# A two-layer encoder's Fourier layer: the place of gate products, norms, spectrum splits and spectrum loads in the queues

## The chip, the core and the metric

One core of a Trainium2 chip runs the whole kernel. The metric is the time of one execution in microseconds on the device, as the median of several runs. The engines are named as in the profile: PE (TensorE, matmuls; PEld is its weight load), DVE (VectorE), ACT (ScalarE), POOL (GpSimd) and SP (SyncE, which here only issues DMAs).

## The reference

Two sequences, x_prompt (2048 x 1024) and x_sample (512 x 1024), go through the same two layers and a final RMSNorm.

```python
def attention_layer(x, ...):                    # layer 0: windowed attention, gated, projected
    h = rmsnorm(x, g)
    z = h @ w_in                                # q, k, v, gate
    o = banded_gqa_with_sink(q, k, v, rel_bias, sink)
    return x + (o * silu(gate)) @ w_out

def fourier_layer(x, g, w_gate, w_out):         # layer 1: the change lies here
    h = rmsnorm(x, g)
    hg = h.reshape(b, s, 4, 256)                # four channel groups
    f = fftn(hg, axes=(1, 3), norm="ortho").real
    gate = h @ w_gate
    return x + (f.reshape(b, s, d) * silu(gate)) @ w_out

# and at the end
return rmsnorm(x, final_norm)
```

All is float32. Matmuls are made of three products of split operands (`matmul3`, L92): high by high, high by low, low by high, where a "split" is a high part copied by ACT and a low part that DVE subtracts.

## The kernel before

The attention layer runs first, up to about 1060 us of the profile, and leaves its result x1 in HBM. The change does not touch it. The Fourier layer, whose first channel DFT starts at 1064.2 us, then runs in these steps.

**Gates.** The 20 tiles of 128 rows are taken in ten pairs (`pairs`). For each pair `gates` (L1104) makes the gate projection of both tiles with seven block products instead of eight, in three PSUM accumulators W, Z and X, and sums them in the SBUF tile c: c11, c12 and c22. Between the products it calls hooks, which do the next pair's transposes, its channel DFT (`z`) and, for the last pair, the first steps of what follows. `silu` (L1115) turns a sum into a gate and POOL stores it to HBM (s2d). At the end of each group of four tiles `combine` runs a radix-4 step over the tiles (L1183) on DVE; the results are the spectra of the positions' first stage, kept in HBM (gsd, evd, odd).

**Positions.** `position` (L1325) is the second DFT stage for one output residue k1. It splits the spectrum (`halves_of`, L1313: two halves of 512 columns, and a real and a sine part for all but k1 = 0 and 8), multiplies it with a table into a cosine sum A and a sine sum B for each half hf, and puts them together on DVE: L1353 to L1356 add and subtract the sine sum. L1356 is the last reader of the sine sum of its half. B has one PSUM bank for both halves, so B's matmuls of the second half wait for L1356 of the first. At the end L1358 multiplies with the gate, 1024 columns at a time, for one or two output tiles (k1 and its mirror).

**Outputs.** `finish` (L1376) transposes the product, projects it with 48 matmuls to two PSUM accumulators (fo), adds them to x1 (L1384) and calls `normed` (L1365): a sum of squares on ACT (L979), a power on POOL (L89), a product of 1024 columns on DVE (L1368), a store on SP. For the last five residues `Outs` (L1389) does the projection with seven products for two tiles, as the gates do: Wo, Zo and Xo, with sums L1449, between which hooks run the next residue's position.

**Order of the work.** The sample (512 rows) comes first: s1 inside the last pair's gates (tiles us, As, Bs), then s0 and s2; then the prompt's residues p0 and p8, p4, p2, p6, p1, p7, p3 and p5. Between them DVE builds the spectra by radix steps (L1181, L1630, L1632): the even ones before p2, the odd ones (g1 to g7) while p2 and p6 run. The spectra of p7, p3 and p5 are stored by ACT (god) and read back by `reads` (L1656) into the tiles go, one residue ahead. A scheduler orders each engine's queue by its own estimate of times and by the dependencies; `after` (L135) gives it a dependency without a semaphore, so that one instruction is placed behind another. So a small edit can move instructions that the diff doesn't name.

The lines and names of the prediction: W, Z, X (gate accumulators), c22 (L1152), us and up (position results of the sample and the prompt), gs and gp (their split spectra), As and Ap, Bs and Bp (cosine and sine sums), tru and tr (transposes), w32f (the output weights as loaded), wo (their split).

Of the kernel before, what the change touches and what calls it, by code (L numbers as in the profile page):

```python
# [42 lines left out]
def encoder(  # L43
# [886 lines left out]
    def fourier_phase(tail):  # L930
        with ExitStack() as es:
# [15 lines left out]
            def zt(name):  # L947
                return right([P, D], F32, name)
# [134 lines left out]
                        ACT.activation(out, v[:, 1], AF.Copy, scale=scale)  # L1083
                        last_z[0] = DVE.scalar_tensor_tensor(out, v[:, 0], scale, out, ALU.mult, ALU.add)

            last_z = [None]

            def prod(out, a, b, ks, first):

# [14 lines left out]
            def gates(pr, hooks):  # L1104
# [44 lines left out]
                hook(3)  # L1149
                x_step(2)  # L1150
                prod(W, S[3], wg["T3"], four, False)
                DVE.tensor_tensor(c22, c22, W, ALU.add)  # L1152
                silu(c22, 1, 1)
                hook(4)
                x_step(3)
# [166 lines left out]
                        out.append(t)  # L1322
                return out

            def position(name, tab, gr, gs, tiles, loads=None, parts=None, between=None):  # L1325

                s2s, tb = loads or position_loads(name, tab, tiles)
                cs, sn, ns = [(tb[:, 2 * i], tb[:, 2 * i + 1]) for i in range(3)]
                bp = bank(f"B{name}")
                us = [zt(f"u{name}_{i}") for i in range(len(tiles))]  # L1330
                for hf in range(2):
                    ts = parts[hf] if parts else halves_of(name, gr, gs, hf)
                    if hf and between:
                        between()

                    def acc(out, tabs, c0, n):
                        for i, (w, t) in enumerate(zip(tabs, ts)):
                            v = [
                                t[:, part].rearrange("p (g c) -> p g c", g=2)[:, :, c0 : c0 + n]
                                for part in range(2)  # L1340
                            ]
                            matmul3(out, w, v, i == 0, i == len(ts) - 1)

                    a = bank(f"A{name}_{hf}")[:, :260].rearrange("p (g c) -> p g c", g=2)
                    acc(a, (cs, ns), 0, 130)
                    b = bp[:, hf * 256 : hf * 256 + 256].rearrange("p (g c) -> p g c", g=2)
                    acc(b, (sn, cs), P, P)
                    uv = [u.rearrange("p (g c) -> p g c", g=4)[:, 2 * hf : 2 * hf + 2] for u in us]
                    ACT.copy(uv[0][:, :, 0 : P + 1], a[:, :, 0 : P + 1])
                    re, im = uv[0][:, :, 1:P], b[:, :, 1:P]  # L1350
                    for v in uv[1:]:
                        ACT.copy(v[:, :, 0 : P + 1 : P], a[:, :, 0 : P + 1 : P])
                        DVE.tensor_tensor(v[:, :, 1:P], re, im, ALU.add)  # L1353
                        DVE.tensor_tensor(v[:, :, P + 1 : 256], re, im, ALU.subtract)
                    DVE.tensor_tensor(uv[0][:, :, P + 1 : 256], re, im, ALU.add)
                    DVE.tensor_tensor(re, re, im, ALU.subtract)  # L1356
                for u, s2 in zip(us, s2s):
                    DVE.tensor_tensor(u, u, s2, ALU.mult)  # L1358
                return list(zip(us, tiles))

            def out_rows(r):
# [3 lines left out]
            def normed(x2, r):  # L1365

                inv = sumsq(x2, f"f{r[0]}")
                DVE.scalar_tensor_tensor(x2, x2, inv[:, 0:1], gfb, ALU.mult, ALU.mult)  # L1368
                SP.dma_start(out_rows(r), x2)

            def residual(r):
# [155 lines left out]
                return name, 4 * k1, gl[0], gl[1] if len(gl) > 1 else None, tiles, (s2s, tb)  # L1527

            POOL.dma_start(mir, mirror)
            first, early, wo, w32f = [], [], [], []  # L1530

            def f_load(k):
                if k < 4:
# [18 lines left out]
            def turn_first(i):  # L1552
# [5 lines left out]
                0: [lambda: f_load(0)],  # L1558
                1: [lambda: f_load(1), lambda: early.append(sample(0, (0,), (left,), (xtile,), left))],
                2: [lambda: f_load(2), lambda: early.append(sample(2, (1,), (left,), (xtile,), left))],  # L1560
                3: [lambda: first.extend(position(*one)), lambda: f_load(3)],
                4: [lambda: f_load(4)],
                5: [lambda: turn_first(0), lambda: f_load(5)],
                6: [lambda: turn_first(1)],
            })
# [14 lines left out]
            G = {}  # L1580
# [59 lines left out]
            g1r, g7r = pm(e0c, o0c, "g1r")  # L1640
            g1s, g7s = pm(o0s, e0s, "g1s")
            g3r, g5r = pm(e1c, o1s, "g3r")
            g5s, g3s = pm(o1c, e1s, "g5s")
            G[1], G[7], G[3], G[5] = (g1r, g1s), (g7r, g7s), (g3r, g3s), (g5r, g5s)
            for k1 in (7, 3, 5):
                for t, g in zip(god[k1], G[k1]):
                    ACT.dma_start(t, g)
            o = Outs(6, position("p6", 6, *G[6], pair(6, 16, 0)))
            f_sums("T1", right)
            f_sums("T2", right)  # L1650
            finish(*pend.pop(0))
# [3 lines left out]

            def reads(k1):  # L1656

                gl = []
                for i, src in enumerate(god[k1]):
                    g = zt(f"go{k1}_{i}")  # L1660
                    SP.dma_start(g, src)
                    gl.append(g)
                return gl, table(f"p{k1}", k1, left)

            nxt = {"r": (G[1], table("p1", 1, left))}
            for k1, k2 in ((1, 7), (7, 3), (3, 5), (5, None)):
# [3 lines left out]
                def split_g():  # L1670

                    nxt["s"] = [gated(name, r, place) for r, place in zip(tiles, (xtile, left))]
                    nxt["p"] = [halves_of(name, *gl, hf) for hf in range(2)]
                    if not ft["T3"]:
                        f_sums("T3", right)

                def transform(third):
                    if not ft["N4"]:
                        f_sums("N4", left)
                    nxt["o"] = Outs(k1, position(name, k1, None, None, tiles, (nxt["s"], tb), nxt["p"], third))  # L1680

                def turns():
                    nxt["o"].operands()
# [108 lines left out]
```

## Time and profile before

| | |
|---|---|
| timed runs | 1588.07, 1588.2, 1588.9 us; median 1588.2 |
| profiled execution | 1587.64 us, its span 1585.9 us |
| granted TensorE clock | 0.999 |
| PE busy | 1572.4 us, 99% of the span |
| DVE, ACT, POOL busy | 1151.0 (73%), 876.4 (55%), 446.5 us (28%) |
| moved by DMA | 373.88 MB, 236 GB/s on average |

The span is the time from the first to the last instruction of the profiled execution; the time of the same execution is a little longer. PE's row says that it has an instruction in work for nearly the whole span. The waits of an engine, listed by who ended them, tell where its remaining idle time comes from, and the timeline gives the start and the duration of each group of instructions, with the idle time before it and what ended it in brackets.

### The profile page before, as it was taken

How to read it: one execution, taken by the hardware profiler on the slowest of the kernel's cores; microseconds unless marked ns; L12 is line 12 of the kernel's file. 1: busy time of each engine (PE TensorE's matmuls, PEld its weight loads, DVE VectorE, ACT ScalarE, POOL GpSimd, SP SyncE). 2: the span in 40 equal slices, each digit the busy share in tenths (PEclk: the TensorE clock that was granted, in tenths of full speed). 3: DMA queues.
4: the chain of work that ended last, by engine and by line, in shares of the span. 5: the costliest groups of instructions: out<-in, count | busy, mean ns of one | idle time of the engine just before them, and what ended most of it. 6: DMA issues, size and time to landing. Idle time of an engine off the chain costs nothing. (4 is left out here: it accounts for less than half of the span.)

```text
span 1585.9 us, 27430 instructions
## 1 busy us (share of the span) xinstructions
PE 1572.4 (99%) x9743; PEld 1320.2 (83%) x9743; DVE 1151.0 (73%) x2785; ACT 876.4 (55%) x2089; POOL 446.5 (28%) x613
## 2 busy tenths in 40 slices
PE   9999999999999999999999999999999999999998
PEld 7778888888898888988888888888888888888886
DVE  5788665887548786378764577669878878889796
ACT  6688634677237684257852476646655554343342
POOL 2566651421403414024222242223112111111110
PEclk9999999999999999999999999999999999999999
DMA  7587696665865567656649656675557469548752
GB/s 288 205 311 282 237 350 211 228 237 199 294 224 205 208 249 257 238 196 229 242 168 334 217 209 225 247 252 199 207 200 262 176 224 406 180 173 313 265 205 80
DMA packets 100579, 373.88 MB, mean 236 GB/s; under 512 B 12139, under 2 KB 22379, under 8 KB 83036
## 3 DMA queue, kind: packets, MB, share of 16 engines
q1 hardware_dynamic: 81708, 297.91, 52.8%
q0 software_dynamic: 16400, 70.04, 11.5%
q10 hardware_dynamic: 2336, 4.20, 0.7%
q8 instruction: 77, 1.26, 0.3%
q14 instruction: 58, 0.48, 0.1%
HBM read 280.84 MB, written 91.26 MB: 235 GB/s over the span
## 5 line engine op out<-in xcount | busy, mean ns | idle before, releaser
L95 PE MATMUL gp<-h,wg 128*128 128x512 f32 x960 | 237.7, 396 | 0.0
L95 PE MATMUL qp<-h,wq 128*128 128x512 f32 x960 | 237.2, 396 | 0.0
L491 DVE CUSTOM_DVE_ANT_0 S<-spt,b 128x385 f32<-128x385 f32 (+1 forms) x320 | 156.5, 528 | 103.7 <-PE spt L472 69.2
L95 PEld LDWEIGHTS gp<-h,wg 128*128 128x128 f32 x960 | 174.9, 188 | 37.3 <-issue 1.0
L95 PEld LDWEIGHTS qp<-h,wq 128*128 128x128 f32 x960 | 174.9, 188 | 36.7 <-issue 0.3
L499 ACT ACTIVATE S<-S 128x385 f32<-128x385 f32 (+1 forms) x320 | 188.8, 596 | 21.0 <-DVE S L491 20.6
L539 ACT CAST pts<-pt 128x384 fp32r<-128x384 f32 (+1 forms) x240 | 101.4, 461 | 166.2 <-PE pt L531 157.5
L540 DVE TENSOR_TENSOR pts<-pt,pts 128x384 fp32r<-128x384 f32 (+1 forms) x240 | 114.7, 524 | 20.5 <-ACT pts L539 19.5
L581 POOL TENSOR_TENSOR uT<-o,uT 128x256 fp32r<-128x256 f32 x75 | 55.6, 741 | 233.1 <-ACT uT L580 233.0
L95 PE MATMUL spt<-wo,uT 128*128 128x512 f32 x480 | 120.4, 391 | 0.0
L472 PE MATMUL spt<-kwin,qab 64*128 64x384 f32 (+1 forms) x960 | 119.1, 353 | 1.2 <-ACT qab L409 0.6
L95 PE MATMUL op<-wo,uT 128*128 128x512 f32 x480 | 118.9, 391 | 0.0
L557 PEld LDWEIGHTS av<-pts,v 128*128 128x128 f32 x576 | 101.3, 188 | 19.2 <-DVE pts L540 0.4
L557 PE MATMUL av<-pts,v 128*128 128x512 f32 (+1 forms) x576 | 116.0, 341 | 0.1
L95 PE MATMUL fo<-wo,tTu 128*128 128x512 f32 x480 | 115.2, 392 | 0.0
L95 PEld LDWEIGHTS op<-wo,uT 128*128 128x128 f32 x480 | 89.4, 188 | 18.5
L95 PEld LDWEIGHTS spt<-wo,uT 128*128 128x128 f32 x480 | 89.1, 188 | 18.4
L95 PEld LDWEIGHTS fo<-wo,tTu 128*128 128x128 f32 x480 | 88.3, 188 | 17.1
L511 DVE TENSOR_SCALAR S<-S 128x384 f32<-128x384 f32 (+1 forms) x192 | 96.0, 500 | 6.8
L472 PEld LDWEIGHTS spt<-kwin,qab 64*128 64x128 f32 x960 | 74.8, 186 | 30.0 <-issue 25.0
L577 POOL TENSOR_TENSOR o<-o,s 128x256 f32<-128x256 f32 x75 | 55.4, 738 | 137.4 <-DVE o L575 137.1
L531 PE MATMUL pt<-ident,S 64*128 64x64 f32 x1344 | 81.8, 222 | 0.0
(321 smaller groups left out, 3185.8 us busy)
## 6 DMA issues: line engine op xcount, KB each, us to landing
wo<-wsd SPq DMA_DIRECT2D x32, 1024.0 KB, 5.6
wq<-wsd SPq DMA_DIRECT2D x31, 1024.0 KB, 7.4
wg<-wsd SPq DMA_DIRECT2D x31, 1024.0 KB, 5.7
x<-x1d SPq DMA_DIRECT2D x40, 512.0 KB, 3.4
b<-b21d SPq DMA_DIRECT2D x40, 512.0 KB, 6.3
b<-rowd SPq DMA_DIRECT2D x40, 384.0 KB, 4.3
xs<-in_x_dram SPq DMA_DIRECT2D x23, 512.0 KB, 6.7
s2d<-gt POOLq DMA_DIRECT2D x40, 256.0 KB, 5.0
```

The costliest lines, as they stand in the source:

```text
L95: pe(PE.matmul(out, a[i], b[j], start=start and i + j == 0, stop=stop and i == 1, skip_group_check=more))
L472: pe(PE.matmul(banks[j][:, 2 + k0 * P : 2 + k1 * P], res["q"][rows, qp, b * P : (b + 1) * P], kwin[g][rows, kp, b * P + k0 * P : b * P + k ...
L491: seq(DVE, DVE.tensor_tensor_reduce(out=s[:, e0:e1], in0=ps[:, 1 + e0 : 1 + e1], in1=st["bias"][:, j, 386 - e1 : 386 - e0][:, ::-1], scale ...
L499: last_exp[0] = seq(ACT, ACT.activation(s[:, e0:e1], s[:, e0:e1], AF.Exp, bias=s[:, 386:387], scale=-1.0, accum_out=s[:, 387:388]))
L511: seq(DVE, DVE.tensor_scalar(s[:, ks], s[:, ks], den, None, ALU.mult))
L531: pe(PE.transpose(ps[h][:, kb, j, :], ss[j][rows, 1 + kb * P : 1 + (kb + 1) * P], ident[rows, rows]))
L539: seq(ACT, ACT.copy(hi, ps[:, k0:k1]))
L540: seq(DVE, DVE.tensor_tensor(lo, ps[:, k0:k1], f32(hi), ALU.subtract))
L557: pe(PE.matmul(to, v, pt, start=n == part == 0, stop=part == 1 and n in (1, len(todo) - 1), skip_group_check=n > 1,))
L577: eng.tensor_tensor(o, o, s, ALU.mult)
L581: low = eng.tensor_tensor(lo, o, f32(hi), ALU.subtract)
```

## The change

Four edits, all in the Fourier layer.

1. The two gate products of s1 (L1358) are no longer written at the end of its position in hook 3 of the last pair's gates. They go to a list, are written in hook 4 behind the sum c22 (L1152), and depend on it in the order of DVE's queue.
2. The norm's product (L1368) depends, in the order of DVE's queue, on the last sine sum (L1356) that was written before it.
3. The first half of p6's spectrum is split before the radix step g5s, not in `position`; and in p1, p7, p3 and p5 the second half is no longer split together with the first but within `position`, after the step that runs between the halves.
4. The spectra of p7, p3 and p5 are read in halves of 512 columns: both tiles' first halves, then both tiles' second halves, four DMAs in place of two.

```diff
-            last_z = [None]
+            last_z, last_c = [None], [None]
...
                 prod(W, S[3], wg["T3"], four, False)
-                DVE.tensor_tensor(c22, c22, W, ALU.add)
+                last_c[0] = DVE.tensor_tensor(c22, c22, W, ALU.add)
...
-            def position(name, tab, gr, gs, tiles, loads=None, parts=None, between=None):
+            last_b = [None]
+
+            def position(name, tab, gr, gs, tiles, loads=None, parts=None, between=None, later=None):
...
                 for hf in range(2):
-                    ts = parts[hf] if parts else halves_of(name, gr, gs, hf)
                     if hf and between:
                         between()
+                    ts = parts[hf] if parts and parts[hf] else halves_of(name, gr, gs, hf)
...
-                    DVE.tensor_tensor(re, re, im, ALU.subtract)
+                    last_b[0] = DVE.tensor_tensor(re, re, im, ALU.subtract)
                 for u, s2 in zip(us, s2s):
-                    DVE.tensor_tensor(u, u, s2, ALU.mult)
+                    if later is None:
+                        DVE.tensor_tensor(u, u, s2, ALU.mult)
+                    else:
+                        later.append(lambda u=u, s2=s2: after(DVE.tensor_tensor(u, u, s2, ALU.mult), last_c[0]))
...
                 inv = sumsq(x2, f"f{r[0]}")
-                DVE.scalar_tensor_tensor(x2, x2, inv[:, 0:1], gfb, ALU.mult, ALU.mult)
+                after(DVE.scalar_tensor_tensor(x2, x2, inv[:, 0:1], gfb, ALU.mult, ALU.mult), last_b[0])
...
-                3: [lambda: first.extend(position(*one)), lambda: f_load(3)],
-                4: [lambda: f_load(4)],
+                3: [lambda: first.extend(position(*one, later=products)), lambda: f_load(3)],
+                4: [lambda: [f() for f in products], lambda: f_load(4)],
...
             g3r, g5r = pm(e1c, o1s, "g3r")
+            p6 = [halves_of("p6", *G[6], 0), None]
             g5s, g3s = pm(o1c, e1s, "g5s")
...
-            o = Outs(6, position("p6", 6, *G[6], pair(6, 16, 0)))
+            o = Outs(6, position("p6", 6, *G[6], pair(6, 16, 0), None, p6))
...
-                gl = []
-                for i, src in enumerate(god[k1]):
-                    g = zt(f"go{k1}_{i}")
-                    SP.dma_start(g, src)
-                    gl.append(g)
+                gl = [zt(f"go{k1}_{i}") for i in range(2)]
+                for hf in range(2):
+                    cs = slice(hf * 512, hf * 512 + 512)
+                    for g, src in zip(gl, god[k1]):
+                        SP.dma_start(g[:, cs], src[:, cs])
...
-                    nxt["p"] = [halves_of(name, *gl, hf) for hf in range(2)]
+                    nxt["p"] = [halves_of(name, *gl, 0), None]
...
-                    nxt["o"] = Outs(k1, position(name, k1, None, None, tiles, (nxt["s"], tb), nxt["p"], third))
+                    nxt["o"] = Outs(k1, position(name, k1, *gl, tiles, (nxt["s"], tb), nxt["p"], third))
```

The arithmetic, the number of matmuls and the bytes moved stay as they are.

More of the change, by code (lines that the diff above doesn't have):

```diff
@@ L1529, in fourier_phase @@
             POOL.dma_start(mir, mirror)
-            first, early, wo, w32f = [], [], [], []
+            first, early, wo, w32f, products = [], [], [], [], []
             def f_load(k):
```

## The prediction

> **What bounds the kernel.** I read the page first, then the waits of TensorE (PE) from 1080 us on, then the timeline of the stretches that the change touches.
>
> ```profile
> span 1585.9 us, 27430 instructions
> PE 1572.4 (99%) x9743; PEld 1320.2 (83%) x9743; DVE 1151.0 (73%) x2785; ACT 876.4 (55%) x2089; POOL 446.5 (28%) x613
> ```
> ```profile
> PE W L95 <- DVE c L1152: 1.0, 1, 1.0
> PE Bp L95 <- DVE up L1356: 0.3, 1, 0.3
> PE Ap L95 <- DVE gp L1321: 0.3, 1, 0.3
> PE Ap L95 <- ACT gp L1320: 0.2, 1, 0.2
> PE Wo L95 <- DVE x L1449: 0.2, 1, 0.2
> ```
>
> PE is busy for 99% of the span and the change leaves its matmuls as they are, so it can win only where PE stands still. In the last 500 us the listed waits make 2.0 us. The list leaves out short idle stretches and the weight load that comes uncovered behind a wait, so each place is priced below by starts of matmuls, at 0.227 us for one of 512 columns (2.72 us for twelve, as 1572.82 to 1575.54 in the stage rows further down). The profiled execution took 1587.64 us, 1.74 more than its span; the median of the three timed runs is 1588.2 (1588.07 to 1588.9). The sum is made against 1587.64 and its difference is taken from 1588.2. "Faster" and "slower" mean by over 0.2%, 3.2 us, about what a measurement of this kernel can tell from no change.
>
> **Part 1: gate products wait for a sum.** DVE's queue here is the last of the sample's sine sums (L1356), the sum c22 (L1152), and two products of 1024 columns (L1358).
>
> ```profile
> 1292.14 1.75 PE L95 MATMUL W<-wT,S 128*128 128x512 f32 x7
> 1293.93 0.69 DVE L1152 TENSOR_TENSOR c<-c,W 128x512 f32<-128x512 f32 x1 [0.45 <-PE W L95]
> ```
> ```profile
> 1318.93 1.76 PE L95 MATMUL W<-wT,S 128*128 128x512 f32 x7
> 1320.20 1.22 DVE L1358 TENSOR_TENSOR us<-us,s2s 128x1024 f32<-128x1024 f32 x1
> 1321.34 0.41 DVE L1356 TENSOR_TENSOR us<-us,Bs 128x254 f32<-128x254 f32 x1
> 1321.66 0.68 DVE L1152 TENSOR_TENSOR c<-c,W 128x512 f32<-128x512 f32 x1
> 1322.40 1.66 PE L95 MATMUL W<-wN,tTb 128*128 128x512 f32 x6 [1.02 <-DVE c L1152]
> ```
> ```profile
> 1327.79 2.20 ACT L1320 CAST gs<-gl 128x512 fp32r<-128x512 f32 x4
> 1328.48 0.39 PE L95 MATMUL As<-gs,tbs 128*128 128x260 f32 x1
> ```
>
> PE waits at 1322.40 for c22, because a product of 1.22 us (1320.20) was put ahead of L1356 and L1152. In the new order of instructions both products stand behind the sum. L1356 then starts at 1320.20, and c22 when W is finished. In the undisturbed pair at 1292 the sum starts 0.43 us after the start of the last of W's seven products (1292.14 + 6 x 0.227 = 1293.50); here that gives 1318.93 + 1.36 + 0.43 = 1320.72. It ends at 1321.40, PE goes on 0.06 us later, as it did in the row, at 1321.46: **0.94 us** gained. Behind the added wait on DVE are the products themselves. The first starts at 1321.3 and ends at 1322.5, and PE asks for it after six products, at 1322.8; the second, after the SiLU step (0.60), ends at 1324.3, and PE asks at 1325.1. Both are hidden by the N4 matmuls; without that cover the second would cost up to its 1.22 us. What is late next is ScalarE's cast for the sample's spectrum (1327.79): the new order has ACT at it 0.69 us sooner and PE one matmul further, 0.92 us together, so the gain passes it.
>
> Behind it the new order gathers the eight transposes of the first result into one group (before: one, three and four of them between matmuls) and moves the second half of the p0 sums behind their release. The uncovered weight loads and short waits there I price at 0.3 us together, between 0 and 0.45. Against that stand the output weights:
>
> ```profile
> 1338.22 1.15 ACT L1548 CAST wo<-w32f 128x512 fp32r<-128x512 f32 x2 [4.02 <-DMA w32f<-in_w_fout_dram]
> ```
>
> That transfer is what ACT waited 4.02 us for. In the new order PE comes to it after 31 long matmuls (7.0 us), 24 short ones and eight transposes (0.12 us each, as six in 0.74: the row at 1467.35 below less the 0.16 that its last one runs over; 3.8 together) from the new As at 1327.79: at 1338.65. If the transfer lands as before, the cast ends at 1338.8, and I take 0.15 us of new wait.
>
> **Part 2: a norm's product behind a sine sum.** This edit names the last sine sum that the program has written down when the norm is written. At p4 and p2 that is the sum of the position before, long past.
>
> ```profile
> 1411.39 1.28 DVE L1368 SCALAR_TENSOR_TENSOR x<-x,invf,gfb 128x1024 f32<-128x1024 f32 x1 [0.41 <-POOL invf L89]
> 1413.06 0.74 PE L95 MATMUL Bp<-gp,tbp 128*128 128x256 f32 x4 [0.26 <-DVE up L1356]
> ```
>
> In the new order L1368 still stands ahead of L1356 at both places. The wait at 1413.06 stays, and this edit is worth 0.
>
> **Part 3: the spectrum of p6 split sooner.** PE stood before the low half of p6's spectrum:
>
> ```profile
> 1435.11 9.25 PE L95 MATMUL fo<-wo,tTu 128*128 128x512 f32 x40
> 1437.54 1.22 DVE L1181 TENSOR_TENSOR g3r<-od,od 128x1024 f32<-128x1024 f32 x1
> 1438.74 1.21 DVE L1181 TENSOR_TENSOR g5s<-tc,od 128x1024 f32<-128x1024 f32 x1
> 1440.40 1.29 DVE L1368 SCALAR_TENSOR_TENSOR x<-x,invf,gfb 128x1024 f32<-128x1024 f32 x1 [0.45 <-POOL invf L89]
> 1441.61 1.22 DVE L1181 TENSOR_TENSOR od<-od,od 128x1024 f32<-128x1024 f32 x1
> 1444.62 0.64 PE L95 MATMUL Ap<-gp,tbp 128*128 128x260 f32 x3 [0.26 <-DVE gp L1321]
> ```
> ```profile
> 1356.98 0.14 DVE L88 TENSOR_SCALAR invf<-ssf 128x1 f32<-128x1 f32 x1
> 1358.17 1.28 DVE L1368 SCALAR_TENSOR_TENSOR x<-x,invf,gfb 128x1024 f32<-128x1024 f32 x1 [0.45 <-POOL invf L89]
> ```
>
> Forty matmuls end at 1444.19, so this wait is 0.43 us. In the new order PE comes to the split after 20 of the 40, and DVE has the norm and one radix step between the first and the second low half. With everything 1.1 us earlier: the first split can start at 1437.6 (after g3r, 1438.7 before) and end at 1438.3; PE is there at 1435.11 + 4.54 - 1.1 = 1438.55. The norm comes 1.19 us after its L88 (1356.98 to 1358.17, also beside a split), at 1438.8; the radix step 1.2 later, at 1440.0; the second split 1.13 after that, ending at 1441.8. PE does six short products (0.73 in all) and nine long ones (2.04) and arrives at 1441.3. So a wait of about 0.5 us takes the place of the 0.43, and I take 0. The bounds are +0.45 (no wait) and -1.1 (DVE's chain of radix steps doesn't follow PE, and all that was won so far is lost here).
>
> **Part 4: spectra in halves.** The four odd stages run the same matmuls, so their starts price the waits at once:
>
> ```profile
> 1467.35 0.90 PE L95 MATMUL Ap<-gp,tbp 128*128 128x260 f32 x6
> 1492.06 0.39 PE L95 MATMUL Ap<-gp,tbp 128*128 128x260 f32 x1
> 1516.84 0.28 PE L95 MATMUL Ap<-gp,tbp 128*128 128x260 f32 x1
> 1540.77 0.28 PE L95 MATMUL Ap<-gp,tbp 128*128 128x260 f32 x1
> ```
> ```profile
> 1572.82 2.88 PE L95 MATMUL Wo<-fT,S 128*128 128x512 f32 x12
> 1575.54 2.88 PE L95 MATMUL Vo<-fN,tT 128*128 128x512 f32 x12
> ```
> ```profile
> 1482.83 0.34 SPq L1369 DMA_DIRECT2D out_dram<-x  x1
> 1483.28 2.01 SPq L1661 DMA_DIRECT2D go<-god  x2
> 1487.97 0.32 SPq L1304 DMA_DIRECT2D s2p<-s2d  x1
> ```
> ```profile
> 1491.39 0.62 ACT L1320 CAST gp<-go 128x512 fp32r<-128x512 f32 x1 [2.65 <-DMA go<-god]
> ```
>
> p1 takes 24.71 us, p7 24.78 and p3 23.93: 0.78 and 0.85 us are lost in the first two, 1.63 together, and that is the ceiling. In p7 the loss begins with the spectrum's landing (1491.39), 8.1 us after its issue. In the new order four half loads stand where two whole ones stood, and ahead of the store of x2_6; ACT's norm sum of x2_10, which stood between the first two casts, goes behind all four. In p1, DVE's sum of x2_10 stands further back and the N4 matmuls that need it are nine products later. By rows like p3's that is a tie, so I keep back 0.3: **1.3 us**. The bounds are 0.5 and 1.63. Six more issues on SP cost nothing, at 0.3 us each (1482.83), since SP computes nothing. The store moved behind them holds the buffer for the load at 1487.97, whose product runs at
>
> ```profile
> 1503.60 1.22 DVE L1358 TENSOR_TENSOR up<-up,s2p 128x1024 f32<-128x1024 f32 x1
> ```
>
> so the load has 15 us from issue to use.
>
> One rule of the skill speaks against this part. The Trainium skill, DMA: Bandwidth & Descriptors, Rules for kernel authors, says to join transfers into large ones. From its table (64 KB 0.95 us, 1 MB 6.15), taken as a line, I estimate 2.0 us for a half and 3.4 for a whole: four halves would land 1.2 us later than two wholes, the first two 2.8 sooner than both wholes. By it the sum would be the same, since only the first pair is waited for. The trace shows transfers of equal size landing very differently, so the rule's effect is a rival below.
>
> **Sum.** 0.94 + 0.3 - 0.15 + 0 + 0 + 1.3 = 2.4 us: 1585.2 against the profiled 1587.64, and **1585.8** against the median.
>
> **Rivals.** *The gain is swallowed at p6.* DVE is nearly full from 1437 to 1444 by the rows above. If its chain keeps its old times, PE's 1.1 us are lost there, and 1.3 stay: 1586.9. For it: every DVE row there follows the one before it. Against: the chain starts with PE's results.
>
> *All touched waits go*, p6's too: 0.94 + 0.45 + 0.43 + 1.63 = 3.45, with small waits of p3 and p5 3.7: 1584.5.
>
> *Halves land no sooner.* These rows are for transfers of 256 KB and 512 KB:
>
> ```profile
> w32N<-sumd SPq DMA_DIRECT2D x8, 256.0 KB, 6.5
> go<-god SPq DMA_DIRECT2D x6, 512.0 KB, 6.7
> ```
>
> If the size doesn't matter, p7's 0.85 stays, and the time is 1588.2 - 2.4 + 0.85 = 1586.6. The rule named above leans this way. Against: the store no longer goes first.
>
> *Slower.* The late store of x2_6 (and of x2_1 and x2_7 in the next stages) releases its buffer late, and the SP queue holds everything behind that load. It decides from the point where the load lands after the product's 1503.60, less the 2.4 won. With the issue at 1488 and landings of 5.1 us (1482.83 to 1487.97) for the store and 6.7 for the load it is there at 1499.8. Were both to take as long as the spectrum's 8.1, it lands at 1504.2, 3.0 late; twice in three stages, 6 - 2.4 = 3.6 us slower, 1591.8.
>
> **How the numbers follow.** The sum as forecast 0.50; p6 swallows 0.18; all waits go 0.16; halves no sooner 0.10; slower 0.06. Faster by over 0.2% needs 3.2 us: most of the third case and a sixth of the first, 0.22. Slower by over 0.2% is the last case with its milder forms left out, 0.05. The rest is 0.73 for within 0.2%. The range goes from the third case, 1584.5, to 1588.5, where nothing is won and the runs lie as high as those shown; it leaves out what lies beyond on both sides.
>
> **What would show it.** Right: the wait for L1152 falls from 1.0 to under 0.3; p1 and p7 each take about 24 us from Ap to Ap; the waits of p4 and p2 for L1356 stay; one wait of about half a microsecond appears at p6 on L1321. Wrong: p6's wait over 1 us, p7 at 24.8, a product L1358 that waits for a transfer, or a difference before 1320 us.

## The result, and the profile after

The changed kernel takes 1585.95 us (median of 22 runs, 1585.46 to 1587.56); the kernel before took 1588.18 beside it (22 runs). The ratio is 0.9986, with a 95% interval of 0.998 to 0.9992: 2.2 us, 0.14% less. Forecast were 1585.8 and "within 0.2%". The sum was right. Two of the four parts from which it was made were not, and the experiments below are mostly about them.

The page of the changed kernel begins with the span and the busy times; below it are all waits of TensorE (PE) from 1080 us on, in the same view as before:

```profile
span 1583.7 us, 27450 instructions
PE 1571.6 (99%) x9743; PEld 1321.7 (83%) x9743; DVE 1150.8 (73%) x2785; ACT 875.7 (55%) x2089; POOL 445.7 (28%) x613
```
```profile
PE Ap L95 <- DVE gp L1321: 0.3, 1, 0.3
PE Bp L95 <- DVE up L1358: 0.2, 1, 0.2
```

Lines behind the change's first insertions carry other numbers now: the last sine sum is L1358 (L1356 before), the gate product L1363 in s1 and L1361 elsewhere (L1358), the norm L1373 (L1368), the loads of a spectrum L1668 (L1661). Five rows of waits with 2.0 us have become two with 0.5. The gates, first on VectorE (DVE), then on PE (start, duration, engine and line):

```profile
1320.27 0.42 DVE L1358 TENSOR_TENSOR us<-us,Bs 128x254 f32<-128x254 f32 x1
1320.71 0.69 DVE L1152 TENSOR_TENSOR c<-c,W 128x512 f32<-128x512 f32 x1
1321.31 1.22 DVE L1363 TENSOR_TENSOR us<-us,s2s 128x1024 f32<-128x1024 f32 x1
...
1320.51 0.84 PE L95 MATMUL X<-b,tTb 128*128 128x512 f32 x3
1321.45 0.73 PE L95 MATMUL W<-wN,tTb 128*128 128x512 f32 x2
```

The sum starts at 1320.71 (forecast 1320.72) and PE goes on at 1321.45 (forecast 1321.46). The four odd stages and the last products:

```profile
1466.40 0.78 PE L95 MATMUL Ap<-gp,tbp 128*128 128x260 f32 x5
1490.23 0.28 PE L95 MATMUL Ap<-gp,tbp 128*128 128x260 f32 x1
1514.33 0.28 PE L95 MATMUL Ap<-gp,tbp 128*128 128x260 f32 x1
1538.44 0.28 PE L95 MATMUL Ap<-gp,tbp 128*128 128x260 f32 x1
1573.45 1.75 PE L95 MATMUL Vo<-fN,tT 128*128 128x512 f32 x7
```

Every stretch of PE work between such rows has the same number of matmuls in each kernel, and the granted clock is 1.00 in all of them but one (halves alone, p7, see there), so its length prices the waits in it. The table gives these lengths in us for both kernels and for those tried below. "N4" runs from the last group of X products to the first N4 product, "to p4" from there to p4's Ap; p4 and p2 are the stretches to the next Ap, p1, p7 and p3 the odd stages, p5 runs from its Ap to the last Vo row. Each line is one profiled execution: the slowest of its kernel's runs for "changed, whole loads", "gates, p6, norm behind the sine sum" and "these three, both", the fastest for "loads ahead of store alone" and "changed, halves split together".

| kernel | N4 | to p4 | p4 | p2 | p6 | p1 | p7 | p3 | p5 |
|---|---|---|---|---|---|---|---|---|---|
| before | 1.86 | 58.40 | 26.83 | 27.12 | 32.60 | 24.71 | 24.78 | 23.93 | 34.77 |
| changed | 0.94 | 58.38 | 26.82 | 27.10 | 32.65 | 23.83 | 24.10 | 24.11 | 35.01 |
| gates alone | 0.94 | 59.63 | 26.83 | 27.07 | 32.61 | 24.46 | 24.44 | 23.93 | 34.82 |
| p6 split alone | 1.84 | 58.54 | 26.82 | 27.09 | 32.60 | 23.84 | 23.93 | 23.91 | 34.91 |
| halves alone | 1.84 | 58.46 | 26.80 | 27.07 | 32.60 | 24.47 | 27.46 | 23.90 | 34.80 |
| halves alone, L88 later | 1.85 | 58.46 | 26.83 | 27.11 | 32.60 | 24.47 | 25.01 | 23.83 | 34.67 |
| loads ahead of store alone | 1.86 | 58.41 | 26.82 | 27.11 | 32.61 | 24.46 | 24.19 | 23.97 | 34.78 |
| changed, whole loads | 0.94 | 59.26 | 26.83 | 27.11 | 32.57 | 23.83 | 24.07 | 24.15 | 35.00 |
| changed, halves split together | 0.94 | 58.37 | 26.83 | 27.11 | 32.58 | 23.80 | 23.91 | 23.97 | 34.86 |
| gates and p6 only | 0.94 | 58.38 | 26.82 | 27.10 | 32.65 | 23.83 | 23.92 | 23.94 | 34.86 |
| gates, p6, norm behind the sine sum | 0.94 | 59.14 | 26.46 | 26.58 | 32.65 | 23.80 | 24.54 | 23.93 | 34.89 |
| these three, weights early | 0.94 | 58.40 | 26.47 | 26.59 | 32.62 | 23.84 | 23.92 | 23.91 | 34.87 |
| these three, L88 later | 0.94 | 58.41 | 26.48 | 26.58 | 32.57 | 23.84 | 23.83 | 23.84 | 34.78 |
| these three, both | 0.94 | 58.37 | 26.46 | 27.74 | 32.61 | 23.83 | 23.83 | 23.77 | 34.78 |

From the first two lines: 0.92 us come from N4, 0.88 from p1, 0.68 from p7; p3 gives back 0.18 and p5 0.24. With 0.02 from "to p4", 0.03 from p4 and p2, -0.05 from p6 and 0.03 by which the changed run was ahead at the X products, that is 2.09, the whole distance between the two Vo rows (1575.54 and 1573.45). Not all of p1's and p7's share is the change's. The kernel with the gates alone has the order of before in these stages and took 24.46 and 24.44: the first tile of p7's spectrum landed at 1490.77 us there, and at 1491.36 in before, where its cast held up the first Ap of p7. Against that line 0.63 and 0.34 are left.

### The profile page after: what moved, and what is told of

Its sections match the earlier page's. It is cut to its first block, busy times and chain, and to the rows that moved or that the text cites. A ratio compares the mean times of both kernels' runs of the same rounds, so it can differ in the third digit from the quotient of the medians.

```text
span 1583.7 us, 27450 instructions
## 1 busy us (share of the span) xinstructions
PE 1571.6 (99%) x9743; PEld 1321.7 (83%) x9743; DVE 1150.8 (73%) x2785; ACT 875.7 (55%) x2089; POOL 445.7 (28%) x613
## 4 chain that ended last, share of the span: by engine, by line
PE 93%; DVE 4%; ACT 2%; issue 1%; DMA 0%; POOL 0%; DVEq 0%; POOLq 0%; SPq 0%; ACTq 0%
PE qp L95 14%; PE gp L95 13%; PE spt L95 11%; PE op L95 7%; PE W L95 6%; PE av L557 6%; PE spt L472 6%; PE fo L95 5%; PE vp L95 3%; PE Wo L95 3%; PE Z L95 3%; PE pt L531 3%; PE z L95 2%; PE Zo L95 2%; PE X L95 2%; PE z L1076 1%
## 5 line engine op out<-in xcount | busy, mean ns | idle before, releaser
L531 PEld LDWEIGHTS pt<-ident,S 64*128 64x128 f32 x1344 | 78.1, 137 | 4.4 <-issue 2.3
```

Of the source, the lines that this page charges most:

```text
L531: pe(PE.transpose(ps[h][:, kb, j, :], ss[j][rows, 1 + kb * P : 1 + (kb + 1) * P], ident[rows, rows]))
```

## The experiments

The medians and ratios are those of each kernel against runs of the kernel before on the same chip; the medians of before were
- 1587.51 for the gates alone, the p6 split alone, the halves alone and the changed kernel with whole loads,
- 1587.61 for the loads ahead of the store, the changed kernel with both halves split together, the gates and p6 split only, and the norm really behind the sine sum,
- 1587.72 for the three kernels with weights early or L88 later, and 1587.31 for the halves alone with L88 behind the split.

### The gates alone

```
...
 for u, s2 in zip(us, s2s):
-    DVE.tensor_tensor(u, u, s2, ALU.mult)
+    if later is None: DVE.tensor_tensor(u, u, s2, ALU.mult)
+    else: later.append(lambda u=u, s2=s2: after(DVE.tensor_tensor(u, u, s2, ALU.mult), last_c[0]))
...
```

> The kernel before with the first edit alone: the two gate products are written behind the sum c22 and wait for it; norm, p6 and spectra as before. The prediction's step 1: TensorE's wait for L1152 at 1322.40 goes (-0.94 us), small waits up to p0 go (-0.3), a new wait for the output weights (+0.15): together -1.1 us, and the stages p1, p7, p3, p5 keep their periods of 24.7, 24.8, 23.9 us. Rival, by the trace of after, in which the lead over before is 0.92 at 1321.45 and 0.98 at 1367.18: the small terms are nothing, -0.95 us, no new wait for the weights. Against both: the lead is lost at p6, as the rival of the prediction had it, then 0 to -0.3 us.

1586.73 us, ratio 0.9997 (0.9988 to 1.0006): not to be told from no change. N4 has its 0.92. The stretch behind it is 1.2 us longer than before, most of it at one place. PE, then ScalarE (ACT):

```profile
1339.74 0.96 PE L95 MATMUL fo<-wo,tTu 128*128 128x512 f32 x3 [1.01 <-ACT wo L1551]
...
1339.08 1.14 ACT L1551 CAST wo<-w32f 128x512 fp32r<-128x512 f32 x2 [1.76 <-DMA w32f<-in_w_fout_dram]
```

This is the new wait for output weights that the prediction priced at 0.15. It was 1.01 here, 0.55 in "changed, whole loads", 0.5 in the first kernel with the moved norm, and nothing in the profiles of the changed kernel and of three others with the same gates and loads. The cast waits for a transfer that landed at 1339.0 here; in the changed kernel the same cast started at 1337.68. Neither expected value (no wait, or 0.15) was right for this run. In the three profiles with the wait PE goes on 0.74 us after the landing (1339.00 to 1339.74 here), and it had asked 17.6 us after its first N4 product (1338.73 here). So the gain at the gates stands whole only if the transfer lands within about 16.8 us of that product: by 1338.3 in the changed kernel, where it landed at 1337.61.

### The p6 split alone

```
 g3r, g5r = pm(e1c, o1s, "g3r")
+p6 = [halves_of("p6", *G[6], 0), None]
 g5s, g3s = pm(o1c, e1s, "g5s")
...
-o = Outs(6, position("p6", 6, *G[6], pair(6, 16, 0)))
+o = Outs(6, position("p6", 6, *G[6], pair(6, 16, 0), None, p6))
```

> The kernel before with the third edit alone: the first half of p6's spectrum is split before g5s is formed; gates, norm and odd spectra as before (whole loads, both halves split together). The prediction's step 3: 0 us (a wait of 0.43 is replaced by one of 0.5), and nothing changes in p1 and p7 (24.7 and 24.8 us). Rival: this edit, not the halves, is what changes the order behind p6: in its built order the store of x2_6 already stands behind the loads of the next spectrum, the norm sum of x2_14 behind all four casts of p1, and six N4 products of p1 behind its Zo products, all of it as in after. Then p1's and p7's waits go with this edit alone: -1.3 to -1.6 us.

1586.10 us, ratio 0.9991 (0.9982 to 1.0000), at the edge of what the runs can tell. The stage starts and SyncE's queue around p7:

```profile
1467.00 0.78 PE L95 MATMUL Ap<-gp,tbp 128*128 128x260 f32 x5
1490.84 0.28 PE L95 MATMUL Ap<-gp,tbp 128*128 128x260 f32 x1
1514.77 0.28 PE L95 MATMUL Ap<-gp,tbp 128*128 128x260 f32 x1
```
```profile
1480.85 0.80 SPq L1662 DMA_DIRECT2D go<-god  x2
1487.10 0.34 SPq L1369 DMA_DIRECT2D out_dram<-x  x1
```

p1 takes 23.84 and p7 23.93 us with whole loads and without any other edit. The rival holds: what the prediction credited to the halves is done here, in the profile by 1.1 us against the stages of the gates alone. At p6 itself the stretch is 32.60, as before, just as the prediction said. But the earlier split shifts what the scheduler does behind it. The norm of x2_6 and its store come later; the two loads, which stood behind that store and were issued at 1483.28, are issued at 1480.85. And in p1 the N4 products come nine products later, so that they no longer wait for VectorE's sum (the 0.2 us on L1449).

### The halves alone

```
-        g = zt(f"go{k1}_{i}")
-        SP.dma_start(g, src)
-        gl.append(g)
+    gl = [zt(f"go{k1}_{i}") for i in range(2)]
+    for hf in range(2):
+        cs = slice(hf * 512, hf * 512 + 512)
+        for g, src in zip(gl, god[k1]):
+            SP.dma_start(g[:, cs], src[:, cs])
...
-    nxt["p"] = [halves_of(name, *gl, hf) for hf in range(2)]
+    nxt["p"] = [halves_of(name, *gl, 0), None]
...
```

> The kernel before with the fourth edit alone: odd spectra loaded as halves, their second half split inside the position; gates, norm and p6 as before. In its built order the store of x2_6 stays ahead of the loads. The prediction's step 4: -1.3 us (p1 and p7 down to about 24 us each). Rival, that the p6 edit did that: p1 keeps 24.7; in p7 the first pair of halves lands sooner than the whole ones did (8.1 us after issue), for up to -0.85; in p3 and p5 the later split of the second half costs 0.2 us each, as the periods of after show (24.1 against 23.9): -0.2 to -0.5 us in all. If neither size nor place of the loads matters: +0.4.

1589.24 us, ratio 1.0015 (1.0006 to 1.0024): slower, which neither theory expected. p1 keeps 24.47, as the rival said; p7 takes 27.46. In its built order ScalarE casts both tiles' first halves and one second half ahead of the sum of squares of x2_10 (jkf), where it had one cast ahead of it before. ACT, DVE and PE:

```profile
1490.08 0.62 ACT L1320 CAST gp<-go 128x512 fp32r<-128x512 f32 x1 [1.63 <-DMA go<-god]
1491.44 1.23 ACT L1320 CAST gp<-go 128x512 fp32r<-128x512 f32 x2 [0.73 <-DMA go<-god]
1492.58 1.05 ACT L979 ACTIVATE jkf<-x 128x1024 bf16<-128x1024 f32 x1
...
1493.75 0.15 DVE L88 TENSOR_SCALAR invf<-ssf 128x1 f32<-128x1 f32 x1 [2.25 <-ACT jkf L979]
1493.82 0.68 DVE L1321 TENSOR_TENSOR gp<-go,gp 128x512 fp32r<-128x512 f32 x1
...
1494.56 0.51 PE L95 MATMUL Ap<-gp,tbp 128*128 128x260 f32 x2 [1.78 <-DVE gp L1321]
1495.26 4.27 PE L95 MATMUL Wo<-fT,S 128*128 128x512 f32 x11
```

The first half did land sooner: its cast starts at 1490.08, against 1491.39 for a whole tile before. Nothing came of it. VectorE's next instruction is L88, one element wide and needed by nobody soon; it waits for ScalarE's sum, which waits for casts, which wait for the second transfer. The split that PE needs stands behind L88 though its own cast was done by 1492.1.

The wait is not all of the loss. Eleven matmuls from 1495.26 to 1499.37 take 4.1 us where eleven of 0.227 take 2.5: from 1495.54 on the granted clock is 0.50 for 3.41 us, which costs about 1.6 us. No other profile here has such a stretch between 7 and 1576 us. It begins 1 us behind the longest wait that PE has in any of these stages; whether the wait brought it about, no run shows.

### The halves alone, with L88 behind the split

```
-nxt["s"] = [gated(name, r, place) for r, place in zip(tiles, (xtile, left))]
 nxt["p"] = [halves_of(name, *gl, 0), None]
+while held: held.pop()()        # the norm of the stage's second row block
+nxt["s"] = [gated(name, r, place) for r, place in zip(tiles, (xtile, left))]
...
-normed(xb, self.us[1][1])
+held.append(lambda: normed(xb, self.us[1][1]))
```

The norm edit of the change is in this kernel too.

> The kernel with the halves alone (fourth edit, nothing else of the change), which had p7 at 27.46 us, with one more edit: the norm of a stage's second row block is written after the splits of the next spectrum's first half. In its built order only VectorE differs: the step L88, which waits for ScalarE's sum of squares of x2_10, stands behind the second split of the first half instead of ahead of it; transfers, casts and matmuls keep their order, and the loads are still behind the store. If L88 at the head of VectorE's queue, and not the transfer itself, is what cost the halves their time: the second split starts when its cast is done, near 1492.1 instead of 1493.8, TensorE's wait of 1.78 us falls to under 0.3, p7 is 25.8 us or less, and the time is 1.5 us or more below that of the halves alone. Rival, the transfer behind the store is simply too late: the wait stays above 1 us.

1588.18 us, ratio 1.0003 (0.9994 to 1.0012). The medians of the two kernels differ by 1.06, or by 0.86 when each is taken against its own runs of before: less than the 1.5 expected. The two stage starts, then VectorE's and PE's rows between them:

```profile
1492.42 0.28 PE L95 MATMUL Ap<-gp,tbp 128*128 128x260 f32 x1
1517.43 0.28 PE L95 MATMUL Ap<-gp,tbp 128*128 128x260 f32 x1
...
1494.73 0.15 DVE L88 TENSOR_SCALAR invf<-ssf 128x1 f32<-128x1 f32 x1 [0.90 <-ACT jkf L979]
...
1494.59 2.69 PE L95 MATMUL Wo<-fT,S 128*128 128x512 f32 x11
1497.12 0.28 PE L95 MATMUL Ap<-gp,tbp 128*128 128x260 f32 x1
1497.58 1.11 PE L95 MATMUL Ap<-gp,tbp 128*128 128x260 f32 x5 [0.18 <-DVE gp L1321]
```

In the profiles of the two kernels TensorE, ScalarE and GpSimd have the same order, and on VectorE only L88 and the norm behind it have moved. The wait of 1.78 falls to 0.10, though the second transfer landed later than in the run above (its cast started at 1492.49, after 2.62 us of waiting). So L88's place made the wait, as expected. p7 falls from 27.46 to 25.01, but not by the wait alone: 1.6 us go with it and its weight load, 1.6 with the half clock, which did not come here, and 0.7 come back at the second half (1497.12 to 1498.52), whose split now stands behind L88.

### The loads ahead of the store, alone

```
-SP.dma_start(out_rows(r), x2)
+after(SP.dma_start(out_rows(r), x2), last_go[0])     # last_go: the spectrum's last load
```

> The kernel before with one edit that is not in the change: the store of a finished position is tied behind the two whole loads of the next odd spectrum, so that the loads are issued first, as they are in after. Loads stay whole, gates and p6 as before. If p7's loss is due to the loads' place behind the store of x2_6: p7 falls from 24.78 to about 24.0 us and p1 keeps its 24.7 or 24.5, together -0.8 us. If the place doesn't matter either (the p6 edit helps by the order of VectorE and ScalarE alone): p7 stays at 24.4 to 24.8, -0.3 to 0 us. The transfers' landing tells: issue to landing of 8.1 us behind the store, then about 1.5 us sooner at least.

1587.54 us, ratio 1.0001 (0.9992 to 1.001): no difference to be measured. In its profile p7 takes 24.19, 0.25 to 0.6 under the 24.44 and 24.78 of kernels with the old order. The loads were issued at 1481.96, 1.3 us sooner than in the profile of before, and ScalarE's second cast still waited until 1490.48 for its transfer. The gain is less than the 0.8 expected, and it is not the place's alone: with the tie the scheduler also put three casts ahead of the sum of squares, not one, and moved a split on VectorE and matmuls of p7. So what the place is worth by itself was not shown.

### The changed kernel with whole loads

```
-    for hf in range(2):
-        cs = slice(hf * 512, hf * 512 + 512)
-        for g, src in zip(gl, god[k1]):
-            SP.dma_start(g[:, cs], src[:, cs])
+    for g, src in zip(gl, god[k1]):
+        SP.dma_start(g, src)
```

> The changed kernel with whole loads of the odd spectra (two of 512 KB where it has four of 256 KB); all else as changed, and the built order of TensorE, VectorE, ScalarE and GpSimd is the same, the loads still ahead of the store. The prediction's step 4 (the size is what helps, p7's 0.85 by it): +0.85 us against the changed kernel, so -1.4 against the kernel before. Rival (the place ahead of the store is what helps): the two transfers are there well before TensorE asks, by the 4 us that the second halves land ahead of it in after (1486.4 against 1490.2): within 0.2 us of the changed kernel, -2.0 to -2.3 against the kernel before, p7 still at 24.1 us.

1585.70 us, ratio 0.9988 (0.9979 to 0.9997). p7 takes 24.07 against 24.10, p3 24.15 against 24.11: inside the change the halves are worth nothing. The rule that the prediction quoted from the Trainium skill (DMA: Bandwidth & Descriptors, Rules for kernel authors: join transfers into large ones) speaks against halves, and these numbers agree with it as far as they go: splitting brought no gain. The prediction's own estimate, the first pair of halves 2.8 us sooner than two wholes, was not borne out: behind the store the second transfer, which completes the pair, landed 7.9 and 8.1 us after its issue in the two kernels with the halves alone, and the second whole 7.8 and 8.3 us in before and in the gates alone.

### The changed kernel with both halves split together

```
-    nxt["p"] = [halves_of(name, *gl, 0), None]
+    nxt["p"] = [halves_of(name, *gl, hf) for hf in range(2)]
```

> The changed kernel with both halves of an odd spectrum split together, as before; the loads stay halves. Built order: TensorE, ScalarE, GpSimd and SyncE as in after; VectorE splits the second half ahead of the sum of the Zo product instead of behind it, at p7, p3 and p5. If the later split is what costs in p3 and p5 (24.11 us against 23.93, and 0.24 from p5 to the end): p3 back to 23.9, p5 to the end 0.2 shorter, p7 perhaps 0.1 shorter, -0.4 to -0.5 us against the changed kernel. If not (one kernel with the later split had p3 at 23.90): no difference within 0.1.

1585.52 us, ratio 0.9987 (0.9978 to 0.9996), which does not differ from the change's 0.9986: the timed runs don't show the 0.4 to 0.5 expected. In the profile p7, p3 and p5 are shorter by 0.19, 0.14 and 0.15, and the changed kernel with whole loads, which splits late too, has p3 and p5 at 24.15 and 35.00. Stage p3 of the changed kernel, DVE and PE, and then the same rows of this one:

```profile
1517.24 0.68 DVE L1454 TENSOR_TENSOR x<-x,Zo 128x512 f32<-128x512 f32 x1
1517.84 1.28 DVE L1321 TENSOR_TENSOR gp<-go,gp 128x512 fp32r<-128x512 f32 x2
...
1518.62 1.06 PE L95 MATMUL Ap<-gp,tbp 128*128 128x260 f32 x6
```
```profile
1516.36 1.29 DVE L1321 TENSOR_TENSOR gp<-go,gp 128x512 fp32r<-128x512 f32 x2
1517.57 0.68 DVE L1454 TENSOR_TENSOR x<-x,Zo 128x512 f32<-128x512 f32 x1
...
1517.75 0.90 PE L95 MATMUL Ap<-gp,tbp 128*128 128x260 f32 x6
```

With the split recorded inside the position, VectorE adds Zo first, and six matmuls take 1.06 us instead of 0.90. No wait is listed for that; only the length of the group shows it. The two kernels with the halves alone also split late and lost nothing in p3 (23.90, 23.83). In the first of them the second of these two splits ends 4.57 us after the stage's first Ap, in the changed kernel 4.79, and there the fifth of the six matmuls, due at 4.78, comes at 4.84. VectorE's order is the same in both, TensorE's is not; why VectorE is 0.2 us later was not followed further.

### Gates and p6 split only

The kernel before with the first and third edit of the change; no norm edit, no halves, both halves split together.

> The kernel before with the first and the third edit only: gate products behind the sum, p6 split sooner; whole loads, halves split together, no norm edit. If these two are the whole gain: N4 0.9 us sooner, p1 23.8, p7 23.9, p3 23.9, and -2.6 us against the kernel before, 0.4 better than the whole change, less whatever TensorE waits for the output weights near 1339 (0 to 1.0 us, by the transfer's landing). If the halves matter: p7 at 24.4 or more and -1.6.

1585.09 us, ratio 0.9986 (0.9977 to 0.9995): 2.52 less than its runs of before, 2.6 expected. Every stretch is as forecast by the two single edits. This is the whole gain of the change, within what the ratios can tell. The norm edit was not run by itself. But the profile of the changed kernel with both halves split together, which has the norm edit and half loads, shows the same order in the Fourier layer on TensorE, VectorE, ScalarE and GpSimd as this one, so there the norm edit moved nothing.

### The norm really behind the sine sum

```
+held = []
...
-after(DVE.scalar_tensor_tensor(x2, x2, inv[:, 0:1], gfb, ALU.mult, ALU.mult), last_b[0])
+held.append(lambda: after(DVE.scalar_tensor_tensor(x2, x2, ..., ALU.mult), last_b[0]))    # and its store
...
 last_b[0] = DVE.tensor_tensor(re, re, im, ALU.subtract)
+while held: held.pop()()        # at p4 and p2: inside the position, behind its first sine sum
```

> The kernel before with the first and the third edit, and the second one done in another way: the norm's product of the last row block of a step is written inside the next position (p4 and p2), behind its first sine sum, and waits for that; so here the norm does stand behind the sine sum on VectorE. If the sine sum is what TensorE waits for at 1385.75 and 1413.06 (before), the waits of 0.26 and 0.43 and the weight loads behind them go: -0.5 to -0.8 us against the same kernel without it, p4 to p2 26.6 and p2 to p6 26.7 us instead of 26.83 and 27.1. Rival: the norm is then late itself, and its store holds the buffer of the next residual's load: no gain, or a new wait of TensorE for x in the next stage.

1584.46 us, ratio 0.9981 (0.9972 to 0.999). p4 falls from 26.82 to 26.46 and p2 from 27.10 to 26.58, 0.88 together; the median is 0.63 below that of the kernel without it, and the intervals overlap. In its profile (1585.71 us, 1.25 above the median) two waits took all of that back: the wait for the weights, listed with 0.5, makes the stretch to p4 0.76 longer, and one in p7 0.62. ACT, DVE and PE:

```profile
1488.53 1.66 ACT L1320 CAST gp<-go 128x512 fp32r<-128x512 f32 x3 [0.69 <-DMA go<-god]
1490.10 1.05 ACT L979 ACTIVATE jkf<-x 128x1024 bf16<-128x1024 f32 x1
...
1491.28 0.15 DVE L88 TENSOR_SCALAR invf<-ssf 128x1 f32<-128x1 f32 x1 [0.69 <-ACT jkf L979]
1491.35 0.68 DVE L1321 TENSOR_TENSOR gp<-go,gp 128x512 fp32r<-128x512 f32 x1
...
1492.09 0.51 PE L95 MATMUL Ap<-gp,tbp 128*128 128x260 f32 x2 [0.46 <-DVE gp L1321]
```

It is the chain of the halves alone: transfer, casts, sum of squares, L88, split, PE. Here too the transfer was late (7.9 us from issue to landing, 6.3 in the kernel without the moved norm), and L88 passed its delay on to a split that had its data.

### Weights early, L88 later, and both

To that kernel were added: the last two weight loads written ahead of p0; the norm of an odd stage's second row block written behind the next spectrum's splits (the edit shown for the halves); and both.

```
+for k in (6, 7):
+    f_load(k)
 new = position(*early[0])
...
-for k in (6, 7):
-    f_load(k)
```

> The kernel with the first and third edit and the norm behind the sine sum at p4 and p2, and one more edit: the last two loads of output weights are written ahead of p0, so that they are issued ahead of the loads of x and of the spectra that stand before them on SyncE's queue. In the runs so far TensorE waited 0, 0.5 or 1.0 us for these weights, as they landed at 1337.6 or at 1339 us. If the wait hangs on the landing alone: no wait for the weights here, the stretch from N4 to p4's Ap 58.4 us in every run as in the changed kernel's (59.1 in the runs with a wait), p7 as before at 23.9 to 24.5. Against the kernel before: -3.2 to -3.6 us. Rival: ScalarE's casts of these weights now stand ahead of the casts for the second result's transposes, which then wait for the transfer: no gain or a wait of the same size in another place.

> The kernel with the first and third edit and the norm behind the sine sum at p4 and p2, and one more edit: in the odd stages the norm of the second row block of a stage is written after the splits of the next spectrum, so that on VectorE its small step L88, which waits for ScalarE's sum of squares, stands behind all four splits instead of ahead of the second one. If L88 at the head of VectorE's queue is what makes TensorE wait in p7 when the spectrum lands late (1.8 us with halves alone, 0.46 with the norm kernel): p7 at 23.9 us in any run, no wait for the split L1321 but that of p6; against the kernel before -3.2 to -3.4 us. Rival: the norms and the stores behind them come 2 us later and hold the buffers of the next residuals: a new wait for x in p3 or p5, or at the end, +0.3 or more.

> Both of the other two kernels' edits together: first and third edit, norm behind the sine sum at p4 and p2, early weight loads, and the norms of the odd stages behind the next splits. If the two waits are independent, their gains add: no wait of TensorE from N4 on but the 0.32 of p6, and -3.6 to -4.0 us against the kernel before, 1.4 or more better than the whole change. If one of the two brings a wait of its own, it lies at the better of the other two kernels.

With early weights 1584.60 us, ratio 0.9978 (0.9969 to 0.9987): the stretch to p4 is 58.40, without a wait, but the median is 3.1 below before's, as without the edit. With L88 later 1583.63 us, ratio 0.9975 (0.9965 to 0.9984), 4.1 below before's where 3.2 to 3.4 were expected: p7 and p3 are at 23.83 and 23.84, among the lowest seen, the end is no longer, and one wait of PE is left from 1315 us on:

```profile
1488.79 2.50 DVE L1321 TENSOR_TENSOR gp<-go,gp 128x512 fp32r<-128x512 f32 x4
1491.20 0.15 DVE L88 TENSOR_SCALAR invf<-ssf 128x1 f32<-128x1 f32 x1
```
```profile
PE Ap L95 <- DVE gp L1321: 0.3, 1, 0.3
```

Both together took 1584.06, ratio 0.9976 (0.9965 to 0.9986): 3.7 below before's and so within the 3.6 to 4.0 expected, but no better than L88 later alone. In its profile (1585.53 us, 1.5 above the median) p2 has a new wait, which makes it 1.16 longer:

```profile
1408.77 0.51 PE L95 MATMUL Ap<-gp,tbp 128*128 128x260 f32 x2 [0.76 <-DVE gp L1321]
```

Whether the early weights push back the spectra that p2's radix steps need was not tried. The best version by the medians is the one with L88 later: 4.1 us less than the kernel before, where the change had 2.2. The two were not timed on the same chip, and their intervals overlap.

## Why the prediction was right in the sum and wrong in its parts

**Part 1, the gates.** 0.94 forecast, 0.92 measured, each step at its time. The 0.3 for small waits was too much: the stretch behind N4 shortened by 0.02. The lead over before, 0.95 at the first N4 product, is 1.04 at the 110th matmul behind it and 0.97 at p4's Ap; what took it back was not followed. The 0.15 for the output weights named the right instruction but not its size: 0 in the profile of the changed kernel, 0.5 to 1.0 in others. TensorE came there later than reckoned, at about 1339.0 and not at 1338.65, so that with the landing of before there would have been no wait. The row of one execution told when that transfer landed there, not how far it moves; it needed bounds, and had none.

**Part 2, the norm.** Right: the built order doesn't change, and the wait before Bp at p2 stays (0.2). Named behind the next position's sine sum instead, the product does what the edit's words say, for 0.88 us.

**Part 3, p6.** Right at its place. Forecast were PE at 1441.3 and the end of the second split at 1441.8. By starts of matmuls PE was there at 1441.46 and went on at 1441.94: 0.48 us where 0.43 was, of which the view lists 0.32 (0.26 before):

```profile
1438.86 1.28 DVE L1373 SCALAR_TENSOR_TENSOR x<-x,invf,gfb 128x1024 f32<-128x1024 f32 x1 [0.44 <-POOL invf L89]
1440.07 1.22 DVE L1181 TENSOR_TENSOR od<-od,od 128x1024 f32<-128x1024 f32 x1
1441.20 0.69 DVE L1321 TENSOR_TENSOR gp<-ev,gp 128x512 fp32r<-128x512 f32 x1
...
1441.94 0.51 PE L95 MATMUL Ap<-gp,tbp 128*128 128x260 f32 x2 [0.32 <-DVE gp L1321]
```

Wrong as the price of the edit: alone it brings 1.4 us by the medians and 1.1 to 1.7 by p1 and p7 (against 24.46 and 24.44, or 24.71 and 24.78).

**Part 4, the halves.** This is the step that failed. "In the new order four half loads stand where two whole ones stood, and ahead of the store of x2_6" was a true reading of the order of the whole change; it was put down to the edit whose lines it shows in. The store's new place, the norm sum behind the four casts and p1's N4 nine products later all come with Part 3. The halves alone cost 1.7 us by the medians' difference (1589.24 against 1587.51), add nothing inside the change, and the later split costs 0.5 in p7, p3 and p5 of the profiles, a term that the prediction did not have. The 1.3 that stood in the sum were near the 1.56 that p1 and p7 gave, for the wrong reason, and that is luck.

**The sum.** 0.92 + 0.02 + 1.56 - 0.42, and 0.01 for the rest, make the profile's 2.09, against 0.94 + 0.3 - 0.15 + 1.3: the small waits missed and the late split's loss stood against a larger gain in p1 and p7.

**The rivals.** The gain did not drown at p6: VectorE's chain follows PE (g3r at 1436.53, 1437.54 before), as argued. "Halves land no sooner" was right in its result for size, but the loss of 0.85 that it priced didn't follow, since p7's wait went by the other edit. The slower rival's premise came true, the store went out at 1486.51 (1482.83 before) and the load behind it at 1489.14 (1487.97), and no product waited for it: the stage's two ran at 1499.26 and 1501.32, 10 and 12 us behind that issue (13.6 and 15.6 in before). Not all touched waits went: 0.5 us are still listed.

## What to carry to other kernels

When a scheduler sets the order, an edit's price isn't at its lines: build each edit alone and compare the orders before the sum is put down to parts, or the sum may be right by accident. On an engine with one queue look for the small instruction that waits for another engine and stands ahead of the one on the critical path; here L88, 0.15 us long, passed a late transfer on to TensorE for 1.8 us, and moving it was worth 0.5 to 0.9 us by the medians in the three pairs of kernels that differ by it. Making the transfer smaller was worth nothing. A gain that ends in front of a transfer's landing needs that landing from several runs, not from one.

## What the runs showed of the hardware that was not expected

The same weight transfer of 512 KB was issued at 1327.36, 1327.59 and 1327.31 in the profiles of before, of the changed kernel and of the gates alone, and landed at 1338.14, 1337.61 and 1339.00: 10.0 to 11.7 us, of which TensorE paid 0 to 1.0. And behind the store of x2_6, the first of four halves landed 7.1 and 5.1 us after its issue in the two kernels with the halves alone, the first of two wholes 8.1 and 7.5 in before and in the gates alone; the second transfer took 7.8 to 8.3 whether half or whole. In this crowded stretch half the size brought only the first transfer in sooner.

In the one profile with a TensorE wait of 1.78 us, the granted clock fell to 0.50 about 1 us behind it, and came back after 3.41 us. Waits of 1.0 us, in the profiles of before and of the gates alone, had no such stretch behind them. Whether the wait was the cause stays open.
